# Priority blocks around the short operations of a recurrence's chunk chain, on one Trainium2 core

## The chip, the core and the metric

The kernel runs on one core of one Trainium2 chip. A core has a matrix engine (TensorE, PE in the profile, with its weight loads as PEld), a vector engine (VectorE, DVE), a scalar engine (ScalarE, ACT), a general engine (GpSimd, POOL) and a queue processor that issues DMAs (SyncE, SP). Each engine runs its own list of instructions; semaphores make one wait for another. The metric is the device time of one execution in microseconds (us), as the median of several runs.

## The reference

One layer of a streaming encoder: 1024 new frames of one stream and 32 frames of a running one, width 2048, float32. Attention with two softmax maps per head and an RWKV-7 recurrence work side by side on the same normed input.

```python
xn = rms_norm(x, norm_g)
proj = xn @ w_in                       # 2048 -> 8320 columns: q, k, v, gates, RWKV r/k/v, LoRA
...                                    # differential attention, chunk mask of 64 frames
def step(S, inp):                      # RWKV-7, one token
    r_t, w_t, k_t, v_t, a_t, b_t = inp
    sa = jnp.einsum('bhij,bhj->bhi', S, a_t)
    S = S * w_t[:, :, None, :] + sa[..., None] * b_t[:, :, None, :] + v_t[..., None] * k_t[:, :, None, :]
    y = jnp.einsum('bhij,bhj->bhi', S, r_t)
    return S, y
...
out = jnp.concatenate([att_out, rw_out], axis=-1) @ w_out
return x + out, k, v, s_final, p_rw[:, -1:]
```

## The kernel before

The frames are worked in two halves: A has 544 columns (512 frames of the new stream and the 32 of the running one), B the other 512. Each half has 8 units, one for a pair of RWKV heads and an attention head, so there are 16 units, and at the end two output projections of 16 blocks each. A unit makes eight column blocks of `xn @ w_in`. `proj` (the tile `pj`) splits weights and inputs into a high and a low float32r part and adds three products, `wh*xh`, `wh*xl` and `wl*xh`. The weights come in groups of 128x512 by DMA from POOL's queue (`wr`, two buffers), ACT casts the high part (`wh`, L234) and DVE subtracts the low part (`wl`, L235), three buffers each; this loading is already in `tc.high_priority()` blocks.

All other work is recorded between these matmuls. Each kind of task (scores, decay, the chain) is a Python generator in a `Stream`; it yields the time after which its next part may be recorded, taken from the table `LAT`, against a clock `clk` that counts planned TensorE time. `pump` runs the streams that are due. What is recorded is then placed by the Tile scheduler: it gives every engine an order of its own, takes from the instructions that it holds ready the one with the earliest place in the recording, and counts time by its own model. An instruction in `tc.high_priority()` goes ahead of others that are ready. So the order on an engine is fixed when the program is built, and at run time each engine takes its list from front to back.

The recurrence is worked in chunks of 64 tokens. `rw_down` prepares a unit's half (`sub` 0 or 1; 4 or 5 chunks): products and masks in `MM`, and 31 steps of a triangular solve on DVE, each a multiply (L803, `tm`) and an add (L805, `ts`). The solve's result goes to DRAM (`dt`) and comes back as `TT` and `t0q`, which DVE transposes to `u0q` (L873); with it `rw_chain` starts its matmuls in the bank `ch`. Then `rw_chain` passes through the chunks one after the other, since each needs the state `Sw` of the one before. A chunk is a chain of four links:

1. PE: `ch<-Sw,AR` (state times rows). ACT copies half of it to `RS` (L927); DVE adds the other half to `MM` as `xs`, in two pieces (L930).
2. ACT makes `SP`, the decayed state (L933, two pieces). PE: `ch<-xs,TT`. ACT and DVE copy one half each to `UV` (L936, L937).
3. PE: `ch<-UV,MM`, twice. DVE makes the new `Sw` in two pieces (L942) and the output `Yt` (L950; L945 for the running stream's chunk).
4. Then the next chunk begins; between the links the generator yields `lat("c1")` to `lat("c3")`.

There are 136 chunks, 128 with `Sw` and 8 of the running stream with `S`. Each kernel matmul in float32 shows as two records in the trace. `ch` is one bank for the whole program.

Of the kernel before, what the change touches and what calls it, by code (L numbers as in the profile page):

```python
# [14 lines left out]
ALU = mybir.AluOpType  # L15
# [31 lines left out]
def build(tc, I, O):  # L47
    nc = tc.nc
    V, S, G, PE = nc.vector, nc.scalar, nc.gpsimd, nc.tensor
# [6 lines left out]
    def T(shape, tag, dt=F32, bufs=1):  # L56
        cnt[0] += 1
        return sb.tile(shape, dt, tag=tag, name=f"{tag}_{cnt[0]}", bufs=bufs)
# [122 lines left out]
    def dma(out, in_):  # L181
        if out.dtype == F32R:
            out, in_ = out.bitcast(F32), in_.bitcast(F32)
        nc.sync.dma_start(out, in_)
# [40 lines left out]
    Spast = dr.tile([NP, 128, 64], F32, name="Spast")  # L225
# [177 lines left out]
    low, high = slice(0, 64), slice(64, 128)  # L403
# [430 lines left out]
    def rw_chain(half, i, sub, st):  # L834
# [4 lines left out]
        AR, MM, MMg, dt, t_m = (st[sub][n] for n in ("AR", "MM", "MMg", "dt", "t_m"))  # L839
# [56 lines left out]
        for q, r, n in quads:  # L896
            h = q % 2
# [14 lines left out]
        for c in order:  # L912
            gc = lo + c
            if c == 4:
                S_ = T([128, 2, 64], "S0")
                G.memset(S_, 0.0)
                for h in range(2):
                    dma(S_[64 * h:64 * h + 64, h, :], I["S0"][i, 64 * h:64 * h + 64, :])
            else:
                S_ = st["Sw"]  # L920
            Sf = S_.rearrange("p h t -> p (h t)")
            yield lat(key, half)
            key = "c1"
            ch = bank("ch")
            mm(ch[:, 0:128], AR[:, c].rearrange("p a t -> p (a t)"), Sf)
            RS = T([128, 128], "RS")
            S.copy(RS[high], ch[high, 0:128])  # L927
            xs = T([128, 64], "xs")
            for h in range(2):
                V.tensor_tensor(xs[64 * h:64 * h + 64], ch[low, 64 * h:64 * h + 64], MM[low, c, h, 0:64], op=ALU.add)  # L930
            SP = T([64, 2, 64], "SP")
            for h, hr in enumerate((low, high)):
                S.activation(SP[:, h, :], S_[hr, h, :], AF.Copy, scale=PL[hr, 0, gc:gc + 1])  # L933
            yield lat("c2", half)
            mm(ch[:, 128:192], TT[:, c, :], xs)
            S.copy(UV[low, c, 0, :], ch[low, 128:192])  # L936
            V.tensor_copy(UV[low, c, 1, :], ch[high, 128:192])  # L937
            yield lat("c3", half)
            for h in range(2):
                mm(ch[:, 192 + 64 * h:256 + 64 * h], MM[:, c, h, 64:192], UV[:, c, h, :])  # L940
            for h, hr in enumerate((low, high)):
                V.scalar_tensor_tensor(S_[hr, h, :], ch[low, 192 + 64 * h:256 + 64 * h], PL[low, h, gc:gc + 1],  # L942
                                       SP[:, h, :], ALU.mult, ALU.add)
            if c == 4:
                V.tensor_tensor(Y[0:64, 2, :], ch[high, 192:320], RS[high], op=ALU.add)  # L945
                G.memset(Y[64:128, 2, :], 0.0)
                for h in range(2):
                    dma(O["wkvs"][i, 64 * h:64 * h + 64, :], S_[64 * h:64 * h + 64, h, :])
            else:
                V.tensor_tensor(Y[64 * (c % 2):64 * (c % 2) + 64, c // 2, :], ch[high, 192:320], RS[high],  # L950
                                op=ALU.add)
                if gc == 7:
                    for h in range(2):
                        dma((Spast, O["wkvp"])[half][i, 64 * h:64 * h + 64, :], S_[64 * h:64 * h + 64, h, :])
        st[sub]["Y"] = Y

    def rw_post(half, i, sub, st):
# [256 lines left out]
```

## Time and profile before

| what | value |
|---|---|
| time, median of 3 runs | 2506.4 us (2506.03 to 2506.7) |
| the profiled execution's own time | 2504.47 us |
| its span, first to last instruction | 2502.7 us |
| PE busy | 2443.2 us, 98% |
| DVE busy | 1864.0 us, 74% |
| ACT busy | 1370.3 us, 55% |
| POOL busy | 453.8 us, 18% |

Busy time is the union of an engine's instructions. The matmuls are pipelined: a record lasts longer than the distance to the next one's start, so a busy PE is not a PE at its peak. An idle time is put down to the instruction that released the wait.

### The profile page before, as it was taken

Reading aid. Unit: us, or ns where it says so; the run is one execution under the profiler, and the core shown is the slowest. Engines: PE = TensorE matmul, PEld = TensorE weight load, DVE = VectorE, ACT = ScalarE, POOL = GpSimd, SP = SyncE. Lnnn points to the kernel's source line nnn. Section 1 sums busy time; section 2 is a strip of 40 time slices with the busy share of each in tenths; the row PEclk is TensorE's granted clock in tenths of the full one; section 3 lists DMA queues with packets and bytes.
Section 4 is the critical chain, followed back from the end, with each engine's and each line's share of the span. In section 5 each row is a group of like instructions: output and inputs, shape, how many; then the busy total and the mean of one; then the engine's idle time right before and its main releaser. Section 6 shows DMA issues by size and latency. Waiting matters only on the chain.

```text
span 2502.7 us, 49026 instructions
## 1 busy us (share of the span) xinstructions
PE 2443.2 (98%) x17124; PEld 2163.9 (86%) x17124; DVE 1864.0 (74%) x5716; ACT 1370.3 (55%) x3286; POOL 453.8 (18%) x1070
## 2 busy tenths in 40 slices
PE   8999999999999999999999999999999999999999
PEld 7999999999999999977777787878787878999887
DVE  7577778788877878778888787878787878643432
ACT  7446465655556665656655565656565656332321
POOL 1212121211212121211111112121211111111100
PEclk9999999999999999999999999999999999999999
DMA  5343333434243525353333333333333344544443
GB/s 181 107 119 90 93 104 96 118 86 120 85 121 123 151 74 149 103 147 94 111 90 95 106 98 103 97 107 90 108 95 109 92 126 146 171 152 136 139 149 104
DMA packets 198919, 286.72 MB, mean 115 GB/s; under 512 B 102352, under 2 KB 116176, under 8 KB 198672
## 3 DMA queue, kind: packets, MB, share of 16 engines
q0 software_dynamic: 51088, 169.12, 22.5%
q1 hardware_dynamic: 147584, 114.47, 16.2%
q8 instruction: 135, 2.21, 0.4%
q14 instruction: 112, 0.92, 0.1%
HBM read 228.11 MB, written 37.51 MB: 106 GB/s over the span
## 4 chain that ended last, share of the span: by engine, by line
PE 69%; DVE 15%; DMA 7%; issue 4%; ACT 4%; POOL 0%; SPq 0%; DVEq 0%; ACTq 0%; POOLq 0%
PE pj L102 54%; PE ch L102 5%; PE am L102 4%; DVE wl L235 3%; PE sc L102 2%; DVE tm L803 2%; DVE ts L805 2%; PE Y L102 2%; DMA wr<-w_in 2%; ACT wh L234 1%; DMA Ks<-t 1%; PE sc L107 1%; PE am L107 1%; DMA p<-wup 1%; DMA wr<-w_out 1%
## 5 line engine op out<-in xcount | busy, mean ns | idle before, releaser
L102 PE MATMUL pj<-xh,wh 128*128 128x288 f32 (+2 forms) x3856 | 1292.4, 335 | 1.9 <-ACT wh L234 1.7
L102 PE MATMUL pj<-xh,wl 128*128 128x288 f32 (+2 forms) x3856 | 1253.4, 325 | 0.1
L102 PE MATMUL pj<-xl,wh 128*128 128x256 f32 (+2 forms) x3856 | 1250.5, 325 | 1.2 <-DVE xl L256 1.2
L102 PEld LDWEIGHTS pj<-xh,wl 128*128 128x128 f32 x3856 | 726.2, 188 | 55.2 <-issue 1.2
L102 PEld LDWEIGHTS pj<-xh,wh 128*128 128x128 f32 x3856 | 727.9, 189 | 53.0 <-ACT wh L234 2.6
L102 PEld LDWEIGHTS pj<-xl,wh 128*128 128x128 f32 x3856 | 728.1, 189 | 45.1 <-DVE xl L256 1.6
L234 ACT CAST wh<-wr 128x512 fp32r<-128x512 f32 x584 | 360.9, 618 | 497.6 <-PE pj L102 431.0
L235 DVE TENSOR_TENSOR wl<-wr,wh 128x512 fp32r<-128x512 f32 x584 | 400.6, 686 | 193.0 <-ACT wh L234 164.4
L241 POOL DMA_DIRECT2D wr<-w_in x517 | 277.9, 538 | 1400.3 <-DVE wl L235 568.7
L803 DVE TENSOR_TENSOR tm<-ts,ms 64x54 f32<-64x54 f32 (+35 forms) x992 | 198.9, 201 | 16.4 <-DMA ts<-tinit 2.3
L805 DVE TENSOR_TENSOR ts<-tm,ts 64x54 f32<-64x54 f32 (+35 forms) x992 | 199.1, 201 | 15.8 <-DVE tm L803 0.3
L933 ACT ACTIVATE SP<-Sw,PL 64x64 f32<-64x64 f32 x256 | 88.3, 345 | 44.2 <-DVE Sw L942 39.0
L235 DVE TENSOR_TENSOR wl<-MM,wh 128x512 fp32r<-128x512 f32 x64 | 44.0, 689 | 88.7 <-ACT wh L234 88.7
L234 ACT CAST wh<-MM 128x512 fp32r<-128x512 f32 x64 | 39.6, 621 | 128.4 <-PE pj L102 124.3
L102 PEld LDWEIGHTS ch<-UV,MM 128*128 128x128 f32 (+1 forms) x1088 | 92.7, 162 | 15.6 <-DVE UV L937 11.1
L102 PE MATMUL ch<-UV,MM 128*128 128x64 f32 (+1 forms) x1088 | 102.6, 246 | 3.5 <-DVE UV L937 3.3
L942 DVE SCALAR_TENSOR_TENSOR Sw<-ch,PL,SP 64x64 f32<-64x64 f32 x256 | 70.5, 275 | 32.1 <-PE ch L102 27.4
L611 ACT ACTIVATE E<-sc,sm 128x640 f32<-128x640 f32 (+3 forms) x64 | 61.0, 954 | 40.3 <-DVE sm L610 40.1
L102 PE MATMUL sc<-Ks,Qd 128*128 128x512 f32 (+2 forms) x224 | 74.1, 342 | 6.5 <-DMA Ks<-t 6.3
L102 PE MATMUL am<-Vt,E 128*128 128x128 f32 (+1 forms) x592 | 79.9, 277 | 0.0
L102 PEld LDWEIGHTS am<-Vt,E 128*128 128x128 f32 (+1 forms) x592 | 71.7, 189 | 5.4 <-ACT E L626 2.0
L930 DVE TENSOR_TENSOR xs<-ch,MM 64x64 f32<-64x64 f32 x272 | 58.2, 214 | 23.6 <-ACT RS L927 19.9
(314 smaller groups left out, 3227.3 us busy)
## 6 DMA issues: line engine op xcount, KB each, us to landing
wr<-w_in POOLq DMA_DIRECT2D x517, 256.0 KB, 3.3
wr<-w_out POOLq DMA_DIRECT2D x64, 256.0 KB, 3.6
MM<-w_out POOLq DMA_DIRECT2D x32, 512.0 KB, 4.2
t<-xB SPq DMA_DIRECT2D x32, 256.0 KB
ms<-dm SPq DMA_DIRECT2D x96, 64.0 KB
t<-t SPq DMA_DIRECT2D x64, 68.0 KB
t<-mixd SPq DMA_DIRECT2D x16, 272.0 KB
t<-xA SPq DMA_DIRECT2D x16, 272.0 KB
```

Source lines behind the costliest of these rows:

```text
L102: PE.matmul(out, lhsT, rhs, start=start, stop=stop)
L107: PE.transpose(out, in_, idn)
L234: S.copy(wh, raw)
L235: V.tensor_tensor(wl, raw, wh.bitcast(F32), op=ALU.subtract)
L241: q.dma_start(raw, wsrc[:, g * 512:(g + 1) * 512].rearrange("p (k f) -> p k f", k=4))
L611: S.activation(E[c][:, :nk], sc[:, :nk], AF.Exp, bias=mx[:, c:c + 1], scale=SCALE, accum_out=l[:, c:c + 1])
L803: V.tensor_tensor(tm, ts_[:, 0:qn, s:s + 1].to_broadcast([R * nb, qn, m]), ms[:, s:s + 1, s + 1:32].to_broadcast([R * nb, qn, m]), op=ALU. ...
L805: V.tensor_tensor(ts_[:, 0:qn, s + 1:32], tm, ts_[:, 0:qn, s + 1:32], op=ALU.add)
L930: V.tensor_tensor(xs[64 * h:64 * h + 64], ch[low, 64 * h:64 * h + 64], MM[low, c, h, 0:64], op=ALU.add)
L933: S.activation(SP[:, h, :], S_[hr, h, :], AF.Copy, scale=PL[hr, 0, gc:gc + 1])
L942: V.scalar_tensor_tensor(S_[hr, h, :], ch[low, 192 + 64 * h:256 + 64 * h], PL[low, h, gc:gc + 1], SP[:, h, :], ALU.mult, ALU.add)
```

## The change

Three `with tc.high_priority():` blocks are put around the chain's short operations: `RS` and `xs`; the two copies to `UV`; the new `Sw` and the output `Yt`. `SP` and the matmuls stay outside. The addition to `Yt` is written once for both kinds of chunk, ahead of the memset that follows it for the running stream. No operation is added or taken away; the lines after move down by up to five (L927 is then L928, L930 L931, L936 and L937 L938 and L939, L942 L945, L950 L948).

```diff
             mm(ch[:, 0:128], AR[:, c].rearrange("p a t -> p (a t)"), Sf)
-            RS = T([128, 128], "RS")
-            S.copy(RS[high], ch[high, 0:128])
-            xs = T([128, 64], "xs")
-            for h in range(2):
-                V.tensor_tensor(xs[64 * h:64 * h + 64], ch[low, 64 * h:64 * h + 64], MM[low, c, h, 0:64], op=ALU.add)
+            with tc.high_priority():
+                RS = T([128, 128], "RS")
+                S.copy(RS[high], ch[high, 0:128])
+                xs = T([128, 64], "xs")
+                for h in range(2):
+                    V.tensor_tensor(xs[64 * h:64 * h + 64], ch[low, 64 * h:64 * h + 64], MM[low, c, h, 0:64], op=ALU.add)
...
             mm(ch[:, 128:192], TT[:, c, :], xs)
-            S.copy(UV[low, c, 0, :], ch[low, 128:192])
-            V.tensor_copy(UV[low, c, 1, :], ch[high, 128:192])
+            with tc.high_priority():
+                S.copy(UV[low, c, 0, :], ch[low, 128:192])
+                V.tensor_copy(UV[low, c, 1, :], ch[high, 128:192])
...
-            for h, hr in enumerate((low, high)):
-                V.scalar_tensor_tensor(S_[hr, h, :], ch[low, 192 + 64 * h:256 + 64 * h], PL[low, h, gc:gc + 1],
-                                       SP[:, h, :], ALU.mult, ALU.add)
+            with tc.high_priority():
+                for h, hr in enumerate((low, high)):
+                    V.scalar_tensor_tensor(S_[hr, h, :], ch[low, 192 + 64 * h:256 + 64 * h], PL[low, h, gc:gc + 1],
+                                           SP[:, h, :], ALU.mult, ALU.add)
+                g, y = (2, low) if c == 4 else (c // 2, (low, high)[c % 2])
+                V.tensor_tensor(Y[y, g, :], ch[high, 192:320], RS[high], op=ALU.add)
             if c == 4:
-                V.tensor_tensor(Y[0:64, 2, :], ch[high, 192:320], RS[high], op=ALU.add)
                 G.memset(Y[64:128, 2, :], 0.0)
...
```

The scheduler then gives other orders on all engines. Three places show it. In the names, the part behind the underscore is a buffer number; `ts` and `tm` are the solve, `ca` the decay's scan, `wl` a weight group's low part.

**First place, DVE, a chunk of unit 6 in half A.** Before, the two pieces of `xs` (one row, x2) stand behind the end of a solve and all scans of the decay:

```order
L805 TENSOR_TENSOR ts_11899<-tm_11985,ts_11899 80x8x3
L549 TENSOR_SCALAR cmb_12500<-cst_251,sx_12495,cvec_68 64x32
L803 TENSOR_TENSOR tm_11988<-ts_11899,ms_11894 80x16
L720 SCALAR_TENSOR_TENSOR ca_12167<-ones_66,ca_12167 128x64
L805 TENSOR_TENSOR ts_11899<-tm_11988,ts_11899 80x8x2
L720 SCALAR_TENSOR_TENSOR ca_12167<-ones_66,ca_12167 128x64
L803 TENSOR_TENSOR tm_11991<-ts_11899,ms_11894 80x8
L720 SCALAR_TENSOR_TENSOR ca_12167<-ones_66,ca_12167 128x64
L805 TENSOR_TENSOR ts_11899<-tm_11991,ts_11899 80x8
L720 SCALAR_TENSOR_TENSOR ca_12167<-ones_66,ca_12167 128x64 x3
L930 TENSOR_TENSOR xs_12530<-ch_1860,MM_11159 64x64 x2
L595 MEMSET sc_286 64x2x64
```

Now the same `xs` stands nine rows behind the `Yt` of the chunk before, and the solve still has ten of its 31 steps to go there:

```order
L948 TENSOR_TENSOR Yt_12387<-ch_1860,RS_12409 64x128
L803 TENSOR_TENSOR tm_11958<-ts_11899,ms_11894 80x60
L472 TENSOR_TENSOR t_12439<-t_12281,Ks_12438 64x544
L235 TENSOR_TENSOR wl_12593<-wr_12590,wh_12592 128x512
L805 TENSOR_TENSOR ts_11899<-tm_11958,ts_11899 80x5x12
L472 TENSOR_TENSOR t_12439<-t_12281,Ks_12438 64x544
L803 TENSOR_TENSOR tm_11961<-ts_11899,ms_11894 80x66
L542 TENSOR_REDUCE sx_12495<-am_274 64x1
L805 TENSOR_TENSOR ts_11899<-tm_11961,ts_11899 80x6x11
L931 TENSOR_TENSOR xs_12530<-ch_1860,MM_11159 64x64 x2
L803 TENSOR_TENSOR tm_11964<-ts_11899,ms_11894 80x60
L543 TENSOR_SCALAR sx_12495<-sx_12495 64x1
```

The chain's pieces moved ahead of the scans and ahead of a part of the solve.

**Second place, PE, the same chunk.** One piece of the difference (- before, + now): where `ch<-Sw,AR` of this chunk stood among the projection's matmuls, the chunk's next link `ch<-xs,TT` now stands.

```order
 L102 MATMUL pj_12567<-xl_22_110,wh_12571 128x288
-L102 MATMUL ch_1860<-Sw_12388,AR_11151 128x128
-L102 MATMUL sc_286<-Ks_12438,Qd_12116 128x128
-L102 MATMUL sc_286<-Ks_12438,Ql_77 128x128
 L102 MATMUL pj_12567<-xh_21_109,wl_12572 128x288
 L102 MATMUL pj_12567<-xh_24_115,wh_12571 128x288
+L102 MATMUL ch_1860<-xs_12530,TT_79 128x64
```

The chain moved forward by about one link against the projection.

**Third place, DVE, the end of the solve of unit 9, `sub` 1, in half B.** Before, a chunk's `xs` stands in two pieces inside the last steps of the solve, and its `UV` behind the end:

```order
L805 TENSOR_TENSOR ts_18980<-tm_19066,ts_18980 64x8x3
L930 TENSOR_TENSOR xs_19645<-ch_1860,MM_18355 64x64
L803 TENSOR_TENSOR tm_19069<-ts_18980,ms_18975 64x16
L610 TENSOR_SCALAR sm_19623<-sm_19623 128x1
L930 TENSOR_TENSOR xs_19645<-ch_1860,MM_18355 64x64
L805 TENSOR_TENSOR ts_18980<-tm_19069,ts_18980 64x8x2
L235 TENSOR_TENSOR wl_19745<-wr_19742,wh_19744 128x512
L803 TENSOR_TENSOR tm_19072<-ts_18980,ms_18975 64x8
L766 TENSOR_TENSOR AR_19843<-rk_19568,P_3177_19277 128x4x64
L805 TENSOR_TENSOR ts_18980<-tm_19072,ts_18980 64x8
L937 COPY UV_18829<-ch_1860 64x64
```

Now no link of the chain is left there; the end of the solve stands behind other rows, among them a row that reads a finished projection bank (L356) and a later weight group:

```order
L805 TENSOR_TENSOR ts_18980<-tm_19066,ts_18980 64x8x3
L803 TENSOR_TENSOR tm_19069<-ts_18980,ms_18975 64x16
L616 RECIPROCAL l_19624<-l_19624 128x2
L805 TENSOR_TENSOR ts_18980<-tm_19069,ts_18980 64x8x2
L617 SCALAR_TENSOR_TENSOR l_19624<-l_19624,cvec_68 128x1
L803 TENSOR_TENSOR tm_19072<-ts_18980,ms_18975 64x8
L356 TENSOR_TENSOR p_3254_19728<-pj_19586,rb_15686 128x8x64
L235 TENSOR_TENSOR wl_19885<-wr_19882,wh_19884 128x512
L805 TENSOR_TENSOR ts_18980<-tm_19072,ts_18980 64x8
L618 SCALAR_TENSOR_TENSOR E_3203_19428<-E_3204_19429,l_19624,E_3203_19428 128x768
```

The chain's links moved ahead of the solve, and the solve's end moved back against the projection.

## Rows read from the trace of the kernel before

**Rows 1.** The page: the span, and the busy time of each engine.

```profile
span 2502.7 us, 49026 instructions
PE 2443.2 (98%) x17124; PEld 2163.9 (86%) x17124; DVE 1864.0 (74%) x5716; ACT 1370.3 (55%) x3286; POOL 453.8 (18%) x1070
```

**Rows 2.** Groups by line: busy us, mean ns | idle before, its releasers.

```profile
L102 PE MATMUL pj<-xh,wh 128*128 128x288 f32 (+2 forms) x3856 | 1292.4, 335 | 1.9 <-ACT wh L234 1.7
...
L102 PE MATMUL ch<-UV,MM 128*128 128x64 f32 (+1 forms) x1088 | 102.6, 246 | 3.5 <-DVE UV L937 3.3
...
L102 PE MATMUL ch<-Sw,AR 128*128 128x128 f32 x256 | 50.9, 280 | 1.5 <-DVE Yt L950 1.3 <-ACT TT L898 0.2
L102 PE MATMUL ch<-xs,TT 128*128 128x64 f32 x272 | 50.0, 265 | 15.1 <-DVE xs L930 9.8 <-ACT sm L388 1.5 <-ACT t L389 1.0
```

**Rows 3.** PE's list of waits: us in total, times, longest.

```profile
PE ch L102 <- DVE xs L930: 9.8, 15, 1.7
...
PE ch L102 <- DVE UV L937: 3.3, 6, 0.9
...
PE pj L102 <- ACT wh L234: 1.7, 1, 1.7
...
PE ch L102 <- DVE u0q L873: 1.1, 1, 1.1
...
PE ch L102 <- ACT TT L898: 0.2, 1, 0.2
```

**Rows 4.** Timeline of PE, unit 6: start, us, what, [idle before].

```profile
869.10 0.28 PE L102 MATMUL pj<-xl,wh 128*128 128x256 f32 x1
869.22 0.28 PE L102 MATMUL pj<-xh,wl 128*128 128x256 f32 x1
870.61 0.41 PE L102 MATMUL ch<-xs,TT 128*128 128x64 f32 x2 [1.11 <-DVE xs L930]
```

**Rows 5.** Timeline of ACT and DVE, the same place.

```profile
867.83 0.26 ACT L927 COPY RS<-ch 64x128 f32<-64x128 f32 x1
...
869.47 0.64 DVE L720 TENSOR_TENSOR_SCAN ca<-ones,ca 128x64 f32<-128x64 f32 x3
...
870.04 0.42 DVE L930 TENSOR_TENSOR xs<-ch,MM 64x64 f32<-64x64 f32 x2
```

**Rows 6.** Timeline of DVE at 2097 us: the two pieces of one `xs`.

```profile
2097.08 0.22 DVE L930 TENSOR_TENSOR xs<-ch,MM 64x64 f32<-64x64 f32 x1
2098.30 0.72 DVE L256 TENSOR_TENSOR xl<-t,xh 128x544 fp32r<-128x544 f32 x1 [1.00 <-ACT xh L255]
2099.06 0.22 DVE L930 TENSOR_TENSOR xs<-ch,MM 64x64 f32<-64x64 f32 x1
```

**Rows 7.** All engines' list of waits, one row of DVE: us, times, longest.

```profile
DVE wl L235 <- ACT wh L234: 253.2, 198, 3.9
```

**Rows 8.** Busy time by stretch: units of half A, of half B.

```profile
330.00:1130.00 800.00, 780.86 (x6520) 740.46 (x6520) 646.77 (x2088) 481.58 (x1235) 156.87 (x410) 1.00 0.39 113
...
1300.00:2090.00 790.00, 780.41 (x4544) 628.83 (x4543) 644.15 (x2028) 475.60 (x1130) 150.72 (x323) 1.00 0.35 101
```

**Rows 9.** Timeline, half A, then half B: a solve's result reaches PE.

```profile
879.05 0.20 DVE L875 STREAM_TRANSPOSE u0q<-t0q 64x32 f32<-64x32 f32 x1
...
891.29 0.38 PE L102 MATMUL ch<-u0q,mq 32*32 32x32 f32 x20
...
1552.60 0.16 DVE L805 TENSOR_TENSOR ts<-tm,ts 64x8 f32<-64x8 f32 x1
...
1562.58 0.39 PE L102 MATMUL pj<-xh,wh 128*128 128x512 f32 x1
...
1562.80 0.40 PE L102 MATMUL pj<-xl,wh 128*128 128x512 f32 x1
...
1562.94 0.23 DVE L873 STREAM_TRANSPOSE u0q<-t0q 128x64 f32<-128x64 f32 x1
...
1563.32 0.33 PE L102 MATMUL ch<-u0q,mq 32*32 32x32 f32 x16
```

More of the change, by code (lines that the diff above doesn't have):

```diff
@@ L940, in rw_chain @@
                 mm(ch[:, 192 + 64 * h:256 + 64 * h], MM[:, c, h, 64:192], UV[:, c, h, :])
-            for h, hr in enumerate((low, high)):
-                V.scalar_tensor_tensor(S_[hr, h, :], ch[low, 192 + 64 * h:256 + 64 * h], PL[low, h, gc:gc + 1],
-                                       SP[:, h, :], ALU.mult, ALU.add)
+            with tc.high_priority():
[4 more added lines that the diff above has]
+                V.tensor_tensor(Y[y, g, :], ch[high, 192:320], RS[high], op=ALU.add)
             if c == 4:
-                V.tensor_tensor(Y[0:64, 2, :], ch[high, 192:320], RS[high], op=ALU.add)
                 G.memset(Y[64:128, 2, :], 0.0)
+            out = O["wkvs"] if c == 4 else (Spast, O["wkvp"])[half] if gc == 7 else None
+            if out is not None:
                 for h in range(2):
[L948 to L954, printed above, removed]
+                    dma(out[i, 64 * h:64 * h + 64, :], S_[64 * h:64 * h + 64, h, :])
         st[sub]["Y"] = Y
```

## The prediction

> **What bounds the kernel now.** I read the page first. PE is busy for 2443.2 of 2502.7 us [rows 1], so nothing but PE's own work and PE's waits sets the time. The change takes no matmul away. What it can win is therefore only what PE loses in waiting for the chain, and what it can cost is new waits of PE. The idle time of the span is 59.5 us (2502.7 - 2443.2), an upper end that no order of work can pass by much.
>
> The groups by line say how much of it belongs to the chain. Ahead of `ch<-xs,TT` PE sits idle for 15.1 us, ahead of `ch<-UV,MM` for 3.5, ahead of `ch<-Sw,AR` for 1.5; ahead of a whole third of the projection's matmuls for 1.9 [rows 2]. PE's list of waits counts them: eleven of its rows are on `ch`, from `xs` (9.8 us in 15 waits) to `TT` (0.2 in one); in all 20.7 us in 32 waits [rows 3]. One of these rows, `u0q` with 1.1 us, is the chain's start after a solve and not one of the links that the change touches. That leaves 19.6 us in 31 waits.
>
> The idle column understates a wait. At 869 us the projection's matmuls start 0.12 us apart, though each lasts 0.28; the last starts at 869.22, the next would have started at 869.34, and `ch<-xs,TT` starts at 870.61 [rows 4]. PE lost 1.27 us, and the row shows 1.11, which is 0.16 less. With 31 x 0.16 = 5.0 us the chain's waits cost about 24.6 us, 1% of the time. Waits shorter than 0.16 us show nowhere; I allow up to 5 us for them in the range.
>
> [...]
>
> Why do the links come late? At the same place `RS` is done at 868.09, and `xs` starts only at 870.04, behind the scans of the decay, which run until 870.1 [rows 5]. PE itself was on time. Two pieces of one `xs` also get separated: at 2097.08 the first runs, then a subtraction for the inputs' low part that had waited 1.00 us for ACT, and the second only at 2099.06 [rows 6].
>
> **The change part by part.** *The blocks around `RS`, `xs`, `UV`, `Sw`, `Yt`.* They remove no work. In the new order both pieces of `xs` follow each other in 133 of 136 chunks, where it was 65; the two pieces of `Sw` in all 136, where it was 55. At the first place the scans now stand behind `xs`. What a link needs at least, with its engines free: `RS` 0.26, `xs` 0.42 for both pieces [rows 5], 0.15 from the end of `xs` (870.46) to the matmul [rows 4, 5], and two hand-overs of the size of that one ahead of `RS` and of `xs`: about 1.1 us.
>
> Against this stands how far PE's order puts `ch<-xs,TT` behind `ch<-Sw,AR`. I count the projection's matmuls between them and take 0.12 us for one of 256 columns [rows 4], 0.13 for 288, and 0.23 for 512 (1562.58 to 1562.80, [rows 9]). The middle chunk keeps its distance, 1.9 us before and after. The long ones go: 45 of 136 had over 2.1 us, now 6. So where the order had put the matmul late because it counted on a late `xs`, both now come early, and a distance of 1.9 us holds 0.8 us over the need. An operation that already runs on DVE or ACT when the link becomes ready takes mostly less (DVE's mean is 1864.0 us over 5716 instructions, 0.33 us [rows 1]).
>
> Short distances stay: under 1.2 us for `xs` 15 chunks, under 0.8 for `UV` 14, under 1.0 for the next `Sw` 8, together 37 links where it was 47. The trace has 31 waits for 47 such links and the late ones together. I take 0.15 us for each of the 37, 5.5 us; the bounds are nothing, and 0.4 us for each, 15 us. Gain from the links: 24.6 - 5.5 = 19.1 us, from 10 to 30.
>
> *What is pushed back: the weights.* Every operation that the links overtake comes later by at most their own time. For the weight split (`wl`) this is off the path: PE waited for weights once in the whole span, 1.7 us [rows 3], while ACT and DVE sit waiting for a free buffer or for each other on 253.2 us of DVE's time [rows 7]. Cover is there, and I cost it at nothing. If it is gone at the one place of a unit where a new column block begins, it costs one link's `xs`, 0.42 us, in 16 units: 7 us.
>
> *What is pushed back: the solve.* This is the real price. `tm` and `ts` are 62 short operations in a row, and their result starts the next chain. In half A there is cover: `u0q` is transposed at 879.05, and PE uses it at 891.29, 12 us later [rows 9]. In half B there is none: `u0q` runs at 1562.94 to 1563.17, PE uses it at 1563.32, and had been free since 1563.03 or so [rows 9]. 13 of the 16 solves of half B look so. In the new order the last step of each `sub` 1 solve there has 6.1 us more DVE work ahead of it (mean durations of the trace for the rows counted), because the links went ahead, and PE's order puts `ch<-u0q` only 20 matmuls of 512 columns later, 4.6 us. Some of the 1.5 us between is paid by links' matmuls that moved ahead of that place on PE too. I take 0.2 us for each of 16, 3.2 us; the bounds are nothing, and 1.5 us for each `sub` 1 solve, 8 x 1.5 = 12 us.
>
> *POOL and SP.* Rows of weight loads and of the solve's transfers trade places with neighbours there, because the instructions that release them move; no transfer is added. Costed at nothing, inside the bounds above.
>
> Sum against the profiled execution: 2504.5 - 19.1 + 3.2 = 2488.6 us. It ran 1.9 us under the median of 2506.4, so for the median **2490 us**, 0.65% less.
>
> **The rivals.** *The waits only change their place (no change).* The middle distance from `Sw` to `xs` is the same 1.9 us before and after, so the links may be as late against PE's order as before, only at other chunks: the half that had been fast stays fast, the others get waits of the old mean, 0.8 us (24.6 / 31). For it speaks that the order is made by a model of time and PE follows at once whatever the model makes early. Against it, that the long waits of rows 4 and 6 each have a named operation in front, which the new order removes. If 25 of 31 waits come back, the gain is 5 us less the solve's 3: 2504 us.
>
> *The solve sets the start of the chains (slower).* DVE works its list from front to back: the second `xs` at 2099.06 could not pass the subtraction that waited 1.00 us [rows 6]. Now the solve's last step stands behind a row that reads a projection bank and behind a weight split, and both wait for other engines. In half B DVE is busy 644.15 of 790 us [rows 8], with little room to catch up. Each us that the 16 chains start later than PE's order has it is a us of PE. The point from which it decides is 19.1 / 16 = 1.2 us a chain; at 2.0 us it costs 32, and the kernel takes 2506 - 19 + 32 = 2519 us. Against it: before, 1.1 us in one wait is all that PE's list shows for `u0q` [rows 3], so the plan and the chip agreed well there.
>
> [...]
>
> That the change doesn't act is not a rival: the orders differ as described.
>
> **How the numbers follow.** Forecast, a gain of 5 to 29 us: 0.72. No change, within 5 us: 0.15. Slower by the solve's start, over 5 us: 0.10. The remaining 0.03 is a gain over 29 us (all waits and the unseen ones go). The low end is 2506.4 - 24.6 - 5.0 = 2477 us. The high end takes the lower bound of the gain, 10, and the upper price of the solve, 12: 2508 us; about 0.15 lies above it and next to nothing below 2477. About 0.2%, 5 us, is what a measurement of this kernel can tell from no change; so faster 0.75, same 0.15, slower 0.10.
>
> **What would show it.** In the profile of the changed kernel: idle ahead of `ch<-xs,TT` down from 15.1 us to under 5, and the rows on `ch` in PE's list from 20.7 to under 8; PE's busy time about unchanged; DVE's time ahead of `xs` and `Sw` waiting for ACT or PE somewhat up. The solve's price would show as waits of PE on `u0q` in half B; the weights' as PE waiting for `wh` or `wl`. The prediction is wrong if the rows on `ch` stay near 20 us, or if they fall and the span doesn't, which would mean that PE waits elsewhere for what was pushed back.

## The result and the profile after

The changed kernel takes **2522.7 us** (median of 4 runs, 2519.6 to 2528.9) against 2506.55 for the kernel before (4 runs, 2506.0 to 2509.8): 1.0067 times as long, with an interval of 1.0051 to 1.0082. It is 16 us slower where 16 us of gain were forecast, and lies outside the range of 2477 to 2508.

The profiled execution took 2519.6 us. The page first, the two lines that answer [rows 1]:

```profile
span 2517.8 us, 49044 instructions
PE 2443.1 (97%) x17124; PEld 2164.3 (86%) x17124; DVE 1869.5 (74%) x5716; ACT 1371.2 (54%) x3286; POOL 455.7 (18%) x1070
```

PE's busy time is what it was, 2443.1 against 2443.2. The span grew by 15.1 us, so all of it is idle time of PE: 59.5 before, 74.7 now. The groups of PE by line (busy us, mean ns, then the idle time just before them and what ended it) say where, to be held against [rows 2]:

```profile
L102 PE MATMUL pj<-xl,wh 128*128 128x288 f32 (+2 forms) x3856 | 1246.9, 323 | 3.6 <-DVE xl L259 2.5 <-DVE xl L256 1.1
...
L102 PE MATMUL ch<-UV,MM 128*128 128x64 f32 (+1 forms) x1088 | 102.2, 246 | 3.3 <-DVE sm L610 1.7 <-DVE UV L939 1.5
...
L102 PE MATMUL ch<-Sw,AR 128*128 128x128 f32 x256 | 50.0, 277 | 0.8 <-ACT TT L898 0.2
...
L102 PE MATMUL ch<-xs,TT 128*128 128x64 f32 x272 | 47.8, 257 | 12.9 <-DVE xs L931 7.2 <-ACT t L389 2.9 <-issue 1.7
...
L107 PE MATMUL sc<-cst,E 128*128 128x128 f32 x288 | 43.1, 275 | 3.8 <-DVE E L618 1.9 <-DVE tm L803 1.6
...
L102 PE MATMUL ch<-u0q,mq 32*32 32x32 f32 x544 | 11.1, 195 | 10.8 <-DVE u0q L873 9.6 <-DVE u0q L875 0.7 <-ACT UV L853 0.3
```

The same groups of the kernel before, where [rows 2] do not have them:

```profile
L102 PE MATMUL pj<-xl,wh 128*128 128x256 f32 (+2 forms) x3856 | 1250.5, 325 | 1.2 <-DVE xl L256 1.2
...
L107 PE MATMUL sc<-cst,E 128*128 128x128 f32 x288 | 46.3, 275 | 1.3 <-DVE E L618 1.2
...
L102 PE MATMUL ch<-u0q,mq 32*32 32x32 f32 x544 | 10.9, 195 | 2.0 <-DVE u0q L873 1.1
```

The links still wait: `xs` 12.9 us instead of 15.1, `UV` 3.3 instead of 3.5, `Sw` 0.8 instead of 1.5. What grew most is `u0q`, from 2.0 to 10.8 us, the transposition of the attention's `E` from 1.3 to 3.8, and `pj<-xl,wh` from 1.2 to 3.6. PE's list of waits (us in total, times, longest), against [rows 3]:

```profile
PE ch L102 <- DVE u0q L873: 9.6, 14, 1.9
...
PE ch L102 <- DVE xs L931: 7.2, 14, 1.7
...
PE ch L102 <- ACT t L389: 2.9, 4, 1.0
...
PE ch L102 <- DVE UV L939: 1.5, 3, 0.6
```

All rows on `ch` together are 27.0 us, where they were 20.7 and the prediction wanted under 8. Without those on `u0q` they are 16.7, where they were 19.6.

Busy time by stretch, for [rows 8] (PE's is the first number after the length):

```profile
330.00:1130.00 800.00, 776.19 (x6489) 735.14 (x6489) 643.13 (x2079) 482.34 (x1228) 152.65 (x408) 1.00 0.39 112
...
1300.00:2090.00 790.00, 772.08 (x4449) 622.24 (x4448) 641.82 (x2013) 464.58 (x1106) 152.06 (x315) 1.00 0.35 100
```

In the units of half A PE is idle for 23.8 us instead of 19.1, in those of half B for 17.9 instead of 9.6.

**Why some links are still late.** Unit 6 again, PE, ACT and DVE in one timeline (start, length, what, [idle before]):

```profile
857.29 0.39 PE L102 MATMUL ch<-Sw,AR 128*128 128x128 f32 x2
...
857.71 0.26 ACT L928 COPY RS<-ch 64x128 f32<-64x128 f32 x1
...
859.72 0.73 DVE L447 TENSOR_TENSOR t<-t,cos 128x544 f32<-128x544 f32 x1
...
860.36 0.68 DVE L235 TENSOR_TENSOR wl<-wr,wh 128x512 fp32r<-128x512 f32 x1
...
860.96 0.44 DVE L931 TENSOR_TENSOR xs<-ch,MM 64x64 f32<-64x64 f32 x2
...
861.50 0.41 PE L102 MATMUL ch<-xs,TT 128*128 128x64 f32 x2 [1.74 <-issue]
```

The `Sw` matmuls start at 857.29, `xs` at 860.96, and it is at high priority. DVE had no gap of more than 0.04 us in between: steps of the solve, two weight splits and a rotation (L447) stand ahead of `xs` in its list. Priority picks among the instructions that are ready in the scheduler's own model of time. So in that model these operations were presumably under way before `xs` was ready; the model's times are not in a trace. On the chip they came later, and DVE took its list in order: from the end of `RS` (857.97) to `xs` it is 2.99 us.

**Why `u0q` is late.** The place of [rows 9] in half B, in the new kernel:

```profile
1566.55 0.16 DVE L805 TENSOR_TENSOR ts<-tm,ts 64x8 f32<-64x8 f32 x1
...
1576.93 0.24 DVE L873 STREAM_TRANSPOSE u0q<-t0q 128x64 f32<-128x64 f32 x1 [0.47 <-DMA t0q<-dt]
...
1577.32 0.33 PE L102 MATMUL ch<-u0q,mq 32*32 32x32 f32 x16 [0.39 <-DVE u0q L873]
```

From the solve's last step to PE it takes 10.8 us, and it took 10.7 in [rows 9] (1552.60 to 1563.32). But the solve itself takes longer. The same solve's stretch by engine, of before and then of after (DVE is the third busy time, with its instructions):

```profile
1517.20:1552.76 35.56, 34.85 (x188) 27.31 (x188) 31.59 (x115) 18.92 (x49) 5.86 (x13) 1.00 0.30 90
```

```profile
1527.80:1566.71 38.91, 38.27 (x195) 30.96 (x195) 36.87 (x132) 20.98 (x51) 7.15 (x15) 1.00 0.30 89
```

DVE does 132 instructions in it instead of 115, and it lasts 3.3 us longer. Between the solve's end and `ch<-u0q` 35 projection matmuls start in the trace of before, and 26 in that of after, 2.1 us less at 0.23 us each. PE's order puts `u0q` 20 of them later, but the solve ends 29 later.

Half A lost cover in the same way. At the place of [rows 9] there, where the transposed result lay 12 us ahead of PE, the new trace has the last piece of the transposition until 894.45 and PE at 894.52. Three more second solves of half A went from 12 to 13 us of cover to 0.15.

At one solve a transfer adds to it. The queue of SP in the new kernel (start, length, what):

```profile
1638.10 3.09 SPq L112 DMA_DIRECT2D t<-t  x3
1641.29 2.51 SPq L184 DMA_DIRECT2D dt<-ts  x4
```

The solve ended at 1640.19; `dt<-ts` stands behind three transfers of the attention's rotation and goes out 1.10 us later. This is one place: behind the other 31 solves of the new kernel it goes out within 0.3 us.

**The whole balance.** The idle column leaves out the short waits that hide under the matmul before: in the new trace a matmul of 512 columns at 1638.44 lasts 0.39 us and the next one starts 0.23 us after it did, so 0.16 us can hide there. I therefore took, for every two matmuls that follow each other, the distance of their starts less the tenth percentile of that distance for the same two shapes over all twenty traces of this study. Only differences between columns mean something. In us, by what stands behind the gap (`ttB` is the due time of the `u0q` step in half B, in the units of the table `LAT`; the last column has it 1200 units later and the priorities of the run `q4_all_tt` below):

| lost ahead of | before | after | before, `ttB`+1500 | after, `ttB`+1500 | after, both cures |
|---|---|---|---|---|---|
| links (`xs`, `UV`, `Sw`) | 74.9 | 62.4 | 79.1 | 54.2 | 53.0 |
| `u0q` | 4.7 | 14.7 | 2.1 | 10.2 | 3.2 |
| scores, `E` | 18.3 | 27.7 | 20.1 | 26.8 | 25.4 |
| `Yt`, `t` at the bank `am` | 6.9 | 9.7 | 11.2 | 12.2 | 12.9 |
| projection | 118.3 | 120.8 | 122.3 | 121.0 | 119.7 |
| all else | 73.9 | 76.7 | 74.9 | 72.6 | 77.5 |
| sum | 296.9 | 311.9 | 309.7 | 297.1 | 291.8 |
| span of the trace | 2502.7 | 2517.8 | 2515.0 | 2502.9 | 2497.2 |

The sums differ as the spans do, within 0.5 us. So the links did win 12.5 us. `u0q` lost 10.0, of which 8.2 in half B, scores and `E` 9.4, the rest 8.1. A single line is less sure than the sum: if only matmuls of the same names count as alike, the links win 9.7, and `u0q` loses 8.9, scores and `E` 13.1. The last three columns belong to the experiments.

### The profile page after: what moved, and what is told of

Read it like the earlier page. It is cut to its first block, busy times and chain, and to the rows that moved or that the text cites. A ratio compares the mean times of both kernels' runs of the same rounds, so it can differ in the third digit from the quotient of the medians.

```text
span 2517.8 us, 49044 instructions
## 1 busy us (share of the span) xinstructions
PE 2443.1 (97%) x17124; PEld 2164.3 (86%) x17124; DVE 1869.5 (74%) x5716; ACT 1371.2 (54%) x3286; POOL 455.7 (18%) x1070
## 4 chain that ended last, share of the span: by engine, by line
PE 68%; DVE 14%; DMA 7%; ACT 5%; issue 3%; SPq 1%; POOL 0%; DVEq 0%; ACTq 0%; POOLq 0%
PE pj L102 53%; PE ch L102 5%; PE am L102 3%; DVE wl L235 3%; PE Y L102 2%; PE sc L102 2%; DVE ts L805 2%; DVE tm L803 1%; DMA Ks<-t 1%; DMA p<-wup 1%; SPq L184 1%; ACT wh L234 1%; PE sc L107 1%; PE am L107 1%; DVE sm L609 1%
## 5 line engine op out<-in xcount | busy, mean ns | idle before, releaser
L102 PE MATMUL pj<-xh,wh 128*128 128x256 f32 (+2 forms) x3856 | 1301.8, 338 | 0.8 <-ACT xh L255 0.8
L102 PE MATMUL pj<-xl,wh 128*128 128x288 f32 (+2 forms) x3856 | 1246.9, 323 | 3.6 <-DVE xl L259 2.5
L102 PEld LDWEIGHTS ch<-UV,MM 128*128 128x128 f32 (+1 forms) x1088 | 93.2, 162 | 16.7 <-DVE UV L939 6.0
L945 DVE SCALAR_TENSOR_TENSOR Sw<-ch,PL,SP 64x64 f32<-64x64 f32 x256 | 70.7, 276 | 21.1 <-PE ch L102 15.8
L931 DVE TENSOR_TENSOR xs<-ch,MM 64x64 f32<-64x64 f32 x272 | 58.6, 215 | 37.1 <-ACT RS L928 33.9
```

The source lines that it names most:

```text
L102: PE.matmul(out, lhsT, rhs, start=start, stop=stop)
```

## The experiments

**One block at a time, and a small shift without priority.** The theories were: (one) links overtake the solve and its transfers, and `u0q` comes too late for PE's order; (two) any new order loses, because the due times were tuned for the old one.

```diff
+            with tc.high_priority():
                 RS = T([128, 128], "RS")
...
```

> Only the first block of the change: the RS copy and the two xs additions of each chunk are issued at high priority; UV, Sw and Y stay as they were. Theory one (the links overtake the solve and the transfers that feed u0q, and TensorE then waits for u0q in the second half): this block carries two of the six VectorE operations of a chunk, so about a third of the added waits, 2506.5 + 5 = 2512 us, with ch<-u0q waits of 4 to 6 us instead of 2.0 and xs waits near the 12.9 us of the full change. Theory two (any new order of an order whose due times were tuned for the old one costs about the same, whatever was moved): 2517 to 2523 us, the full change's loss, with the added waits scattered over many consumers. The prediction's own account (the links' waits go and nothing is given back): 2506.5 - 10 = 2496 us.

Measured: 2514.0 us, ratio 1.0035 (1.0021 to 1.0049).

```diff
+            with tc.high_priority():
                 S.copy(UV[low, c, 0, :], ch[low, 128:192])
                 V.tensor_copy(UV[low, c, 1, :], ch[high, 128:192])
```

> Only the second block of the change: the two UV copies (one on ScalarE, one on VectorE) of each chunk are issued at high priority. Theory one (the solve and the u0q transfers are overtaken): one VectorE operation of a chunk, about a sixth of the loss, 2506.5 + 2 = 2509 us, u0q waits 2 to 4 us. Theory two (any new order costs the same): 2517 to 2523 us. The prediction's account: the UV waits were 3.5 us, so 2503 us.

Measured: 2506.0 us, 1.0006 (0.9995 to 1.0018).

```diff
+            with tc.high_priority():
                 for h, hr in enumerate((low, high)):
                     V.scalar_tensor_tensor(S_[hr, h, :], ...
...
```

> Only the third block of the change: the two Sw updates and the Y addition of each chunk are issued at high priority. Theory one (the solve and the u0q transfers are overtaken): three VectorE operations of a chunk, the largest part of the loss, 2506.5 + 8 = 2514 us, with ch<-u0q waits of 6 to 9 us. Theory two (any new order costs the same): 2517 to 2523 us. The prediction's account: the Sw waits were 1.6 us, so 2505 us, or up to 3 us less where the Y addition also comes earlier to the post-processing.

Measured: 2521.6 us, 1.0065 (1.0052 to 1.0077).

```diff
-c1A=2400, c1B=2200, c2A=1800, c2B=1800, c3A=1350, c3B=1500
+c1A=2500, c1B=2300, c2A=1900, c2B=1900, c3A=1450, c3B=1600
```

> The kernel before without any high priority; instead every due time of the chain's three stages is raised by 100 units in the table LAT, which shifts the fixed order of all engines a little and has nothing to do with the solve. Theory one (the loss comes from links overtaking the solve and its transfers): no more than a few us either way, 2503 to 2511 us, u0q waits as before (2.0 us), because links are not put ahead of the solve. Theory two (the kernel before sits at a tuned point and any new order loses): 2513 to 2523 us, slower by about as much as the change.

Measured: 2503.5 us, 0.9989 (0.9980 to 0.9999).

Theory two falls as it was put: two new orders lose nothing. The sizes go as theory one had them, small for `UV`, middle for `xs`, largest for `Sw`, but more than it allowed for the last two, and its reason holds in part for `xs` and not for `Sw`. PE's waits with the first block alone:

```profile
PE ch L102 <- DVE UV L938: 10.3, 22, 0.8
...
PE ch L102 <- DVE u0q L873: 4.2, 7, 0.8
...
PE ch L102 <- DVE xs L931: 2.9, 4, 1.7
```

`u0q` rises to 4.2 us, as theory one had it, but that is 2 us of some 9. `xs` falls to 2.9 us, and `UV`, the next link, rises from 3.3 to 10.3. With the third block alone:

```profile
PE ch L102 <- DVE xs L930: 10.1, 26, 1.0
...
PE pj L102 <- DVE xl L259: 4.5, 1, 4.5
...
PE sc L107 <- DVE E L618: 4.2, 8, 2.1
...
PE ch L102 <- DVE u0q L873: 2.1, 6, 1.1
```

Here `u0q` costs 2.1 us in all, where theory one had 6 to 9, and the waits are at a projection matmul at the start of half B (4.5 in one), at `E` and at `xs`. So a block that is moved ahead makes others late, and which ones depends on the block.

**The solve's priority, the transfers' priority, and longer distances for the links.**

```diff
+        with tc.high_priority():
             for s in range(31):
...
```

> The changed kernel, with the 31 steps of the solve in VectorE (two operations each) at high priority as well, so that the links no longer overtake the solve there. Theory one (the solve ends later, so u0q comes later than TensorE's fixed order has it): u0q waits of TensorE fall from 10.8 to 2 to 4 us and the time by 7 to 9 us, to about 2514. Theory two in its new form (what the chain gains is paid by whatever stands next in VectorE's queue, the solve being only one of them): the u0q waits fall too, but others grow (xs, UV, weights, normalization), and the time stays at 2519 to 2525 us.

Measured: 2522.4 us, 1.0053 (1.0039 to 1.0067); two of six runs near 2514, with a granted clock of 0.997 where the others had 0.994 to 0.996. `u0q` hardly moved:

```profile
PE ch L102 <- DVE u0q L874: 8.9, 13, 2.0
```

The solve's stretch (DVE is the third busy time):

```profile
1523.80:1562.37 38.57, 38.00 (x195) 30.96 (x194) 36.77 (x131) 20.98 (x51) 7.18 (x15) 1.00 0.30 89
```

131 instructions of DVE in 38.57 us are what the changed kernel has without that priority (132 in 38.91). Each step of the solve needs the step before, and as many operations stand between the steps.

```diff
+        with tc.high_priority():
             for s in range(31):
...
+        with tc.high_priority():
             for w in range(R):
                 dma(dtv[w], ts_[w * nb:(w + 1) * nb])
...
+        with tc.high_priority():
             for b in range(2):
                 for h in range(2):
                     o = 64 * h + 32 * b
                     dma(TT[o:o + 32, :, o:o + 32], dtg[b, h, 0:32])
...
+        with tc.high_priority():
             whole(V.transpose, u0, t0.rearrange("p j t -> p (j t)"))
```

(the `t0q` and `t1q` transfers too)

> The changed kernel, with the solve's 31 steps, the transfers that follow it on SyncE's queue (ts to dt, dt to TT, t0q and t1q) and the transposition to u0q at high priority. Theory one with the transfers as the larger part (in the changed kernel the dt transfer was held 1.1 us behind three rotation transfers in SyncE's queue): u0q waits below 2 us, 2508 to 2512 us, 2 to 5 us better than with the solve alone. If the queue did not matter, the same time as with the solve alone. Theory two (what is put first is paid by the next in line): 2519 us or more.

Measured: 2507.8 us, 1.0002 (0.9993 to 1.0011). The loss is gone, though 4.9 us of `u0q` are left in six waits, where under 2 were expected:

```profile
PE ch L102 <- DVE xs L936: 7.2, 12, 1.7
...
PE ch L102 <- DVE u0q L877: 4.9, 6, 1.4
```

```diff
-c1A=2400, c1B=2200, c2A=1800, c2B=1800
+c1A=3400, c1B=3200, c2A=2500, c2B=2500
```

> The kernel before without any new high priority, with the due times of the first two stages of the chain raised (c1 by 1000 units, c2 by 700) so that TensorE's fixed order puts more other matmuls between a link's matmul and the next. It asks what the links' waits are worth when they are taken away without giving VectorE's queue another order of preference. If the waits are worth what the prediction said: xs waits fall from 15.1 to under 5 us, and the time by up to 10 to 15 us, to 2491 to 2497. If the chain's length is what holds (34 chunks in a row per pair of units, each then longer by 1.7 us): the last units and the post-processing come late, and it is 2506 us or slower, with new waits of am<-cst,Yt and u0q.

Measured: 2528.1 us, 1.0096 (1.0081 to 1.0111). More distance didn't buy the links' waits: `xs` is still at 8.6 us, and PE waits 10.7 us ahead of `am<-cst,Yt` where it was 3.1, most of it for `MM`.

```profile
PE am L107 <- DVE MM L784: 9.6, 8, 2.7
PE ch L102 <- DVE xs L930: 8.6, 14, 1.7
```

> The kernel before with only the solve's 31 steps at high priority, no links. It is the control for the changed kernel with the solve at high priority: it tells what the solve's priority does by itself. Theory one: the solve was in time before (u0q waits 2.0 us), so 2503 to 2508 us, with at most 2 us of the u0q waits gone and the links' waits a little larger. Theory two (what is put first is paid by the next in line): xs waits grow from 15.1 to 20 us or more and the time is 2510 us or more.

(the same block around the 31 steps, in the kernel before) Measured: 2504.4 us, 0.9989 (0.9981 to 0.9998). The priority of the solve alone does little in either kernel, some 3 us.

**The transfers alone, a later due time, and the halves.**

> The changed kernel with only the transfers behind the solve (ts to dt, dt to TT, t0q and t1q) and the transposition to u0q at high priority; the solve's own steps as in the changed kernel. With the solve and the transfers both at high priority the loss was gone (2508), with the solve alone it was not (2514 to 2523). Theory one, transfers: 2506 to 2511 us, u0q waits 4 to 7 us, the solve's priority adds nothing. Theory one, both needed together: about 2515 to 2520 us.

(the blocks around the transfers and the transposition, without that around the solve) Measured: 2513.2 us, 1.0021 (1.0011 to 1.0030), between the two forecasts. About 10 of 16 us come back; the two priorities mend more together than apart. The way from the solve's end to the transposition, as the median of the 12 solves that start between 1340 and 2050 us, was 10.2 us before and 11.0 in the changed kernel; here it is 9.5. So the priority doesn't only take back what the change had added, it makes the way shorter than it was.

```diff
-ttB=24000
+ttB=25500
```

> The changed kernel, no further priority; the due time of the u0q step in the second half is raised by 1500 units in the table LAT, so that TensorE's fixed order has the u0q matmuls later, by about the lateness of u0q in the trace (0.3 to 1.9 us). Theory one (TensorE waits for a late u0q and nothing else pays): the u0q waits of the second half (5.7 us between 1300 and 2090 us) go, and the time falls by 4 to 8 us, to 2515 to 2519. If the chain behind u0q is what is late, its start is moved by as much, and links, normalization and post-processing wait instead: 2521 us or more.

Measured: 2504.7 us, 0.9993 (0.9984 to 1.0002). One number in the table of due times brings back all 16 us and 2 more, over twice what theory one had allowed. And it isn't `u0q` alone that mends: in the table 8.2 us come back ahead of the links and 4.5 ahead of `u0q`. The orders of the other engines change too. The second solve of a unit, which had 132 instructions of DVE, has 107 in a shorter stretch:

```profile
1650.50:1681.86 31.36, 30.95 (x175) 26.02 (x176) 28.34 (x107) 17.07 (x44) 4.93 (x10) 1.00 0.24 69
...
PE ch L102 <- DVE u0q L873: 5.7, 8, 1.1
```

> The kernel before with the solve, its transfers and the transposition at high priority, and no links. It is the same set as in the kernel that brought the changed kernel back to 2508, on the kernel before. If the transfers' priority is a gain of its own that has nothing to do with the links (so that the change would still cost 15 us beside it): 2490 to 2495 us. If it only takes back what the links did: 2502 to 2507 us, with u0q waits of 1 us.

(all the solve and transfer blocks, in the kernel before) Measured: 2501.8 us, 0.9987 (0.9977 to 0.9997): a gain of its own of some 3 to 5 us, not of 15. The way from the solve's end to the transposition is 8.9 us in it.

```diff
-            with tc.high_priority():
+            with tc.high_priority() if half == 0 else ExitStack():
...
```

(the same at all three blocks)

> The three blocks of the change at high priority in the first half of the sequence only; the chains of the second half as before. By the marks of the two traces, the first half lost 4 to 5 us up to 1080 us (3.0 of them in unit 6) and the second half 9 more. Theory one (the loss is that of u0q in the second half, where TensorE's order has no time to spare): 2507 to 2512 us with u0q waits of 2 to 4 us. Theory two (the new order pays wherever it is): about half the loss in each half of the sequence, 2514 us or more.

Measured: 2510.3 us, 1.0012 (1.0002 to 1.0023). Half A's part is about 3 of the 16 us. The rest is half B's by difference; no run has the blocks in half B alone.

**The controls.** The later due time could have been a gain in any order. Its trace was not a clean witness either, with 5.7 us of `u0q` left in eight waits.

> The kernel before, no new priority, with only the due time of the u0q step in the second half raised by 1500 units, as in the run that brought the changed kernel back to 2505. If the later u0q step cures what the change made late, then the kernel before, where u0q was in time, gains nothing from it: 2504 to 2512 us. If the raised due time is worth 15 us by itself (another order of TensorE's matmuls, 9.7 us less matmul time in the second half): 2490 to 2495 us, and the change still costs its 15 us beside it.

(`ttB=25500` in the kernel before) Measured: 2520.4 us, 1.0057 (1.0043 to 1.0071), 14 us slower, outside both forecasts. Here `u0q` is ready long before PE comes to it, the solve's last step, the transposition and PE again:

```profile
1548.05 0.17 DVE L805 TENSOR_TENSOR ts<-tm,ts 64x8 f32<-64x8 f32 x1
...
1556.29 0.20 DVE L873 STREAM_TRANSPOSE u0q<-t0q 128x64 f32<-128x64 f32 x1
...
1563.43 0.33 PE L102 MATMUL ch<-u0q,mq 32*32 32x32 f32 x16
```

6.9 us lie between the end of the transposition and PE, where there were 0.15 in [rows 9]. The chains start later than they could. In the table above 4.2 us more are lost ahead of the links, 4.3 ahead of `Yt` and `t`, which stand behind the chains' ends, 4.0 ahead of the projection and 1.8 ahead of the scores. **The same 1500 units cost 14 us before the change and bring 18 after it.** Read the other way: at `ttB=24000` the change costs 16 us, at 25500 it wins 0.64% (1.0057 to 0.9993), 16 us.

> The kernel before with only the third block of the change (Sw and Y), and the solve, its transfers and the transposition at high priority. The third block alone cost 16 us with hardly more u0q waits than before (2.7 us). If its loss is the same thing as the change's (what stands behind the links in the queues comes late, the solve's result first): 2505 to 2510 us. If its loss is other waits (the first matmuls of a unit for xh and xl, the xs link, and a lower granted clock behind them): it stays at 2517 to 2522 us.

(the third block alone, with the solve and transfer blocks) Measured: 2515.0 us, 1.0036 (1.0024 to 1.0048). 6 to 7 of the 16 us of this block come back, less than the one forecast and more than the other. PE's waits for `u0q` are not what came back: they are 4.1 us here and were 2.1. I have no run that takes the rest away.

> The changed kernel with both cures together: the solve, its transfers and the transposition at high priority, and the due time of the u0q step in the second half raised by 1200 units. In the run with the priorities alone, u0q waits of 4.6 us were left between 1300 and 2090 us, about 1 us in one chain of each unit. If these are lost time: 2501 to 2504 us, better than either cure and than the kernel before. If the cures mend the same thing: 2504 to 2509 us.

(the solve and transfer blocks, and `ttB=25200`) Measured: 2500.3 us, 0.9980 (0.9971 to 0.9989), **faster than both kernels**. `u0q` is down to 0.3 us:

```profile
PE ch L102 <- DVE xs L936: 5.8, 12, 1.7
...
PE am L107 <- DVE Yt L976: 5.1, 9, 0.8
PE ch L102 <- ACT MM L895: 4.5, 7, 1.1
...
PE ch L102 <- DVE u0q L877: 0.3, 1, 0.3
```

New are waits on `MM` and on `Yt`, the ends of the chains.

> The kernel before with the solve, its transfers and the transposition at high priority (2502 us alone) and with the chain's due times raised by 100 units (2504 us alone), no link at high priority. If both small gains add: 2498 to 2501 us. If any order near the tuned one comes out within a few us at random: 2501 to 2510 us.

Measured: 2501.8 us, 0.9978 (0.9968 to 0.9988). The median lies just above the forecast for gains that add. By the ratios they do add: 0.9987 and 0.9989 make 0.9976. The interval is too wide to tell this from either gain alone. But this is a version without any link at high priority that is about as fast as the cured kernel with them (0.9980). **Set best against best, the links' priority has shown no gain here that is clear of the intervals.**

**The scores.** The table's line on scores and `E` stays at 25 to 28 us in its three kernels with the change, the cures included, where it was 18.3.

```diff
-att0A=4044, att0B=1900, scAA=7000, sc2B=4200
+att0A=4644, att0B=2500, scAA=7300, sc2B=4500
```

> The changed kernel with both cures (priority for the solve, its transfers and the transposition; the u0q step of the second half due 1200 units later), and now the attention scores due later too: the first block of a head by 600 units, the transposition of E by 300. In all kernels with the change, TensorE's losses ahead of the scores were 8 to 13 us over those of the kernel before, also where the cures had brought the rest back. If these are lost to due times that are too early for the new order, as with u0q: 2490 to 2496 us. If the attention's later end makes others late in turn (final normalization, the next head): 2500 us or more.

(on top of both cures) Measured: 2499.7 us, 0.9964 (0.9951 to 0.9976), also faster than both kernels, and the lowest ratio of the study. The scores' line of the table doesn't fall (26.0 after 25.4); the interval overlaps that of the kernel with both cures, and the forecast of 2490 to 2496 is missed.

> The kernel before, no new priority, with the same later due times of the scores (600 and 300 units). The control: if the scores' due times fit the kernel before, as that of u0q did, it gets slower, by 5 to 15 us (2511 to 2521 us). If later scores are a gain in any order: 2500 us or less.

(these due times in the kernel before) Measured: 2513.1 us, 1.0018 (1.0009 to 1.0027), 5 us slower. Again the due times fit the kernel before; but in the changed kernel later ones didn't take the scores' loss away.

## Why the prediction was wrong

**The bound and the size of the waits: right.** PE's busy time is unchanged, and the time is PE's own work and PE's waits. Hidden parts of waits count, as the prediction said, and more than it allowed: by the idle column the links won 3.1 us, by the distances of starts 12.5.

**The gain of the links, 19.1 us: the mechanism was right, the size was not.** In the changed kernel they gave 12.5, near the lower bound of 10; with the later due time of `u0q` 21 to 22 (table, last two columns against the first). The failed assumption is that operations which stand together, and early, in the order run early on the chip. At 860.96 us `xs` stands behind operations that the chip had not reached. The prediction named the long waits' cause ("behind the scans") and held it removed; another operation took their place.

**The weights, at nothing: about right.** The projection's line grew from 118.3 to 120.8 in the table; PE waited 2.5 us for `xl`, which is not a weight, at the start of half B.

**The solve, 3.2 us: the right place and too low.** The prediction counted 6.1 us more DVE work against 4.6 us that PE's order gave back. The trace has 29 projection matmuls against 20, much the same. It then took 0.2 us a chain out of bounds of 0 to 12 us in all; measured were 10.0 us, 8.2 of them in half B, half a us for each of its 16 chains, as short waits and hidden ones. Cover had been 0.15 us at each such place [rows 9], and the prediction itself saw 13 of 16 so: nothing there supported the low end. And the cover that it counted on in half A, 12 us, was read from a trace of the old order; in the new one it is gone at that place and three more.

**POOL and SP, at nothing: wrong in part.** `dt<-ts` stood 1.10 us behind rotation transfers at one place, and the priority of transfers and transposition brought back some 10 us. With the solve's priority the same blocks gave the kernel before 3 to 5 us, so part of this isn't a loss taken back.

**What the sum left out is the larger part, and this is the step that failed.** The prediction asked what stands behind the links and answered with weights and solve only; all else that shares DVE, ACT and SP with the links it put at nothing by not naming it. Scores and `E` lost 9.4 us, `Yt`, the projection and the rest 8.1. With 10.0 for `u0q` that is 27.5 us lost against 12.5 won, where the sum had 3.2 against 19.1. That due times fitted to the old order are behind it is shown for `u0q` (the same 1500 units help one kernel and hurt the other); for scores and `E` it is not.

**The rivals.** "The solve sets the start of the chains" gave 2519 us for 2.0 us a chain. The place is one of the right ones, but half a us a chain is under its own point of decision, 1.2 us: by its own sum the kernel would have been faster, and that its time is close is luck. What it had for it, an order of instructions that nothing passes, shows at 860.96 on DVE (2.99 us) and at 1641.29 in SP's queue (1.10 us). "The waits only change their place" describes the first block's run best: `xs` fell by 7 us, `UV` rose by 7.

**The granted clock.** The profiled runs of before and after both show 0.998, so the 15 us of the traces owe it nothing. The other three runs of after had 0.995 to 0.996, which goes with 3 to 9 us more than the profiled one. In the third block's run it is a larger part: its five runs had 0.994 to 0.996. Stretches of its trace, PE's busy time first and the clock third from the end, the matmuls at the first of them, and the lowest such stretch of before:

```profile
1080.00:1090.00 10.00, 5.54 (x18) 4.46 (x18) 8.11 (x22) 5.08 (x11) 1.07 (x2) 0.83 0.60 198
...
2140.00:2150.00 10.00, 10.00 (x58) 9.49 (x59) 7.15 (x25) 3.24 (x10) 1.08 (x2) 0.70 0.48 160
```

```profile
1079.64 0.40 PE L102 MATMUL pj<-xh,wh 128*128 128x512 f32 x1
1084.51 0.80 PE L102 MATMUL pj<-xl,wh 128*128 128x512 f32 x1 [4.46 <-DVE xl L259]
```

```profile
290.00:300.00 10.00, 9.14 (x42) 7.91 (x43) 5.86 (x24) 2.49 (x5) 0.54 (x1) 0.66 0.28 86
```

In the new trace the 288-column matmuls start 0.13 us apart at 818 us, at a granted clock of 1.00, and 0.24 at 823 to 825, at 0.50. By that I estimate what the missing clock costs as its share of the time: summed over all stretches of 10 us below full clock, 10.2 us there and 5.1 in the trace of before. By this estimate up to 5 us of that block's loss is clock. One of its falls comes right behind the 4.46 us at 1084: the matmul after it lasts 0.80 us, and the one ahead of it 0.40. The longest, 0.96 in the stretch from 2130 and 0.70 in the one from 2140, has no single wait of that size in the first of them (PE was busy for 7.77 of its 10 us).

**What stays open:** why scores and `E` lose 7 to 9 us in the kernels with the change; later due times for them didn't take it away. And 9 of the 16 us of the third block alone.

## What to carry to other kernels

Where one engine's order is fixed by planned times, a priority on another engine is a change of plan: retune the due times of what stands behind it in the same queues before judging it. The change cost 16 us with the old table and won 16 against the same kernel at a due time 1500 units later. But judge by the best of either side: without any link at high priority a little tuning reached 0.9978, with the links and both cures 0.9980, and with later scores as well 0.9964; the intervals overlap. Read the margin at each hand-over first; where result and user are 0.15 us apart, as `u0q` and PE were, there is no cover. A margin of 12 us is no cover either if it comes from the order that is about to change. A priority for a chain of dependent steps did little here, some 3 us; one for the transfers that carry its result and the transposition brought back about 10 of the 16.

## What was not expected of the hardware

How little of the short waits shows as idle time of PE: the links won 12.5 us by the distances of starts, and 3.1 by the idle column. And the clock: in the trace of the third block, after PE had been idle for 4.46 us until 1084.51, the granted clock of the 10 us around it was 0.83, and the next matmul lasted 0.80 us where the one ahead of the wait had lasted 0.40.
